# A hybrid decoder block on one core: first input piece in one transfer, 12 idle products, another order list, another order of squares at the join

## Chip, cores and metric

The kernel runs on one core of one Trainium2 chip. The metric is the device time in microseconds of one execution, as the median of the runs. The core's engines are TensorE (PE; its weight loads are shown as PEld), VectorE (DVE), ScalarE (ACT), GpSimd (POOL) and SyncE (SP), which here issues nearly all transfers.

## What is computed

One decoder layer in float32 on x of 256 tokens by 1024. The reference, cut to its frame:

```python
for l in range(DEPTH):                     # DEPTH = 1
    h = rms_norm(x, mix_pre_norm[l])
    mix = hybrid_token_mixer(h, w_in[l], ..., w_out[l], ...)
    x = x + rms_norm(mix, mix_post_norm[l])
    h = rms_norm(x, ffn_pre_norm[l])
    x = x + rms_norm(conv_glu_ffn(h, w_up[l], ffn_conv_w[l], ffn_conv_b[l], w_down[l]), ffn_post_norm[l])
```

The mixer projects h once and splits the columns into three groups of heads: sliding-window attention with sinks, block attention (one block of 256 here, so plain causal attention with ALiBi), and a gated delta rule with a short convolution on q, k and v, whose chunk needs the inverse of a unit lower triangular matrix. The three outputs are joined and go through w_out. The feed-forward part is up-projection (2 x 2816 columns), a convolution of width 3, GeGLU and down-projection.

## The kernel before

**Split products.** Every large product is made of three: each operand is split into a high part (rounded to the type fp32r, by ACT) and a low part (the rest, by VectorE), and hi x hi, hi x lo and lo x hi are summed in PSUM (`passes`). So each weight that arrives must be cast by ACT and then subtracted by VectorE before TensorE can use it.

**The start.** SP loads the transposed x together with the first weights (values of both attentions and the gates, 392 columns) in four pieces `fx[0]` to `fx[3]`, each with two of the eight k-tiles; `fx[0]` comes in two transfers, one per k-tile (L206, L207), the others whole (L209). The norm's weights `pre` come by their own transfer on ACT's queue (L200). While they are on the way TensorE runs WARM = 16 products of a tile of ones with itself (`idle`, L282), whose result nobody reads. Then, for each k-tile, ACT makes the high part of x times `pre` (L292) and of the weights (L293), VectorE the low parts (L294, L296), and TensorE sums them into `pb` (L302), k-tiles 0 and 1 first, then 2 and 3, and so on.

**The mixer.** The rest of the mixer is written as short generators: `n` is the first norm (its last product `p_r`, L331, and the copy `rbc`, L333, which every projection's evacuation needs), `g0` to `g11` are the delta rule's projections (four steps of 6 products, L354, then evacuation, convolution and tanh), `a0` to `a6` those of the attentions, `z0` and `z1` the output gates, `lX` loads of weights and `sX` their splits (L223 and L227; `so` are those of w_out), `i` and `j` the two parts of the triangular inverse (short, dependent steps on VectorE, ACT and TensorE), `r`, `f`, `w`, `s`, `u` the delta rule's products with it, `o0` and `o1` its outputs with their norm, `p`, `N`, `T` and `v` scores, normalising, turning and the value products of the attentions, `t` the turning of the delta rule's outputs, `O` the products of w_out: `O8` is its k-tile 4 for the first 128 tokens, and the two steps of one O are the two halves of 512 columns. A list of 645 steps, PLAN, says in which order these steps are issued; `g0*2` means two steps of g0. Under the manual schedule each engine works its instructions off in the order of that list, so a step that waits holds up what stands behind it on its engine. Some last steps of w_out (`w_rest`) are held back to fill the join.

**The join.** When all of w_out for the first 128 tokens is summed in two halves `pm[0][0]` and `pm[0][1]`, ACT squares each half and sums the squares (`post_sq`, L988), VectorE multiplies it by the norm's weights (`post_w`, L991); `resid` makes the root (`rms_scale`: the sum's scaling L87 and L89, ACT's root L91, the reciprocal L95), adds x, squares again, and `norm_transpose` weighs and turns the result (L164), on which the up-projection starts. Then follows the same for the other 128 tokens.

**The feed-forward part** (`load_up`, `up_products`, `up_gate`, `down`) streams 33 MB of weights. It isn't touched.

## Time and profile before

| | us |
|---|---|
| median of 3 runs (336.42 to 336.85) | 336.52 |
| profiled execution | 335.96 |
| its span, first to last instruction | 334.20 |

| engine | busy us | share of the span |
|---|---|---|
| PE | 321.7 | 96% |
| PEld | 296.4 | 89% |
| DVE | 264.0 | 79% |
| ACT | 212.8 | 64% |
| POOL | 2.4 | 1% |

The profile is that of one execution. The busy share is a mean over stages that have different limits, so it is read by stage: which engine is full in a stretch, and which wait ends last there. An instruction's row gives its start, how long it took, the engine, the line, the operation with the tiles written and read, and in brackets how long the engine stood idle before it and what ended that. Matmuls overlap: one that took 0.39 us may follow the one before by 0.23 us. A plain float32 product of 128 columns is recorded as two matmuls, a transpose as one. The granted clock was 0.993 of full speed as a mean.

### The profile page before, as it was taken

How to read it: one execution, taken by the hardware profiler on the slowest of the kernel's cores; microseconds unless marked ns; L12 is line 12 of the kernel's file. 1: busy time of each engine (PE TensorE's matmuls, PEld its weight loads, DVE VectorE, ACT ScalarE, POOL GpSimd, SP SyncE). 2: the span in 40 equal slices, each digit the busy share in tenths (PEclk: the TensorE clock that was granted, in tenths of full speed). 3: DMA queues.
4: the chain of work that ended last, by engine and by line, in shares of the span. 5: the costliest groups of instructions: out<-in, count | busy, mean ns of one | idle time of the engine just before them, and what ended most of it. 6: DMA issues, size and time to landing. Idle time of an engine off the chain costs nothing.

```text
...
## 1 busy us (share of the span) xinstructions
PE 321.7 (96%) x2500; PEld 296.4 (89%) x2500; DVE 264.0 (79%) x596; ACT 212.8 (64%) x457; POOL 2.4 (1%) x11
## 2 busy tenths in 40 slices
...
GB/s 271 420 354 273 102 233 126 127 93 99 25 355 240 15 140 347 79 127 49 206 127 232 334 315 246 176 210 250 128 234 146 251 127 126 127 126 2 0 61 64
DMA packets 9821, 58.18 MB, mean 174 GB/s; under 512 B 1472, under 2 KB 1728, under 8 KB 3520
## 3 DMA queue, kind: packets, MB, share of 16 engines
...
q10 hardware_dynamic: 144, 0.00, 0.0%
...
## 4 chain that ended last, share of the span: by engine, by line
PE 59%; DVE 26%; ACT 8%; DMA 3%; issue 2%; SPq 1%; DVEq 0%; ACTq 0%
PE pu L181 29%; PE py L187 17%; PE pm L187 7%; DVE cv L372 4%; PE pt L1005 3%; DMA wg_raw<-wg 3%; DVE wg_lo L227 3%; DVE wa_lo L227 2%; DVE u L1036 2%; DVE wz_lo L227 1%; DVE cm L366 1%; ACT wo_hi L223 1%; DVE pr L875 1%; DVE wd_lo L121 1%; DVE U L610 1%
## 5 line engine op out<-in xcount | busy, mean ns | idle before, releaser
L181 PE MATMUL pu<-hT_hi,wu_hi 128*128 128x256 f32 x304 | 84.3, 277 | 0.0
L181 PE MATMUL pu<-hT_lo,wu_hi 128*128 128x256 f32 x304 | 84.1, 277 | 0.0
L181 PE MATMUL pu<-hT_hi,wu_lo 128*128 128x256 f32 x304 | 84.1, 277 | 0.0
L121 DVE TENSOR_TENSOR wu_lo<-wu_raw,wu_hi 128x1024 fp32r<-128x1024 f32 (+1 forms) x54 | 51.7, 983 | 19.8 <-ACT wu_hi L120 19.8
L181 PEld LDWEIGHTS pu<-hT_lo,wu_hi 128*128 128x128 f32 x304 | 57.2, 188 | 0.7
L181 PEld LDWEIGHTS pu<-hT_hi,wu_hi 128*128 128x128 f32 x304 | 57.1, 188 | 0.7
L181 PEld LDWEIGHTS pu<-hT_hi,wu_lo 128*128 128x128 f32 x304 | 57.1, 188 | 0.0
L120 ACT CAST wu_hi<-wu_raw 128x1024 fp32r<-128x1024 f32 (+1 forms) x54 | 44.7, 858 | 16.9 <-PE pu L181 16.9
L1036 DVE SCALAR_TENSOR_TENSOR u<-pu,prm,u 128x255 f32<-128x255 f32 (+1 forms) x88 | 41.1, 477 | 6.3 <-ACT u L1034 5.2
L187 PE MATMUL py<-wd_hi,mT_hi 128*128 128x512 f32 x88 | 34.4, 391 | 0.2 <-ACT wd_hi L120 0.2
L187 PE MATMUL py<-wd_hi,mT_lo 128*128 128x512 f32 x88 | 34.5, 392 | 0.0
L187 PE MATMUL py<-wd_lo,mT_hi 128*128 128x512 f32 x88 | 34.3, 394 | 0.0
L131 ACT CAST mT_hi<-ge 128x256 fp32r<-128x256 f32 x22 | 8.9, 406 | 32.8 <-DVE ge L1040 32.8
L121 DVE TENSOR_TENSOR wd_lo<-wd_raw,wd_hi 128x1024 fp32r<-128x1024 f32 (+1 forms) x28 | 27.1, 987 | 1.3 <-ACT wd_hi L120 1.3
L1034 ACT ACTIVATE u<-pu,prm 128x256 f32<-128x256 f32 x44 | 24.2, 560 | 5.4 <-PE pu L181 5.4
L120 ACT CAST wd_hi<-wd_raw 128x1024 fp32r<-128x1024 f32 (+1 forms) x28 | 22.8, 865 | 2.9 <-DMA wd_raw<-wd 2.9
L354 PE MATMUL pg<-hT_hi,wg_hi 128*128 128x256 f32 x96 | 24.1, 287 | 0.2 <-ACT wg_hi L223 0.2
L354 PE MATMUL pg<-hT_lo,wg_hi 128*128 128x256 f32 x96 | 23.2, 277 | 0.0
L187 PEld LDWEIGHTS py<-wd_hi,mT_hi 128*128 128x128 f32 x88 | 16.5, 188 | 3.4 <-ACT wd_hi L120 0.4
L187 PEld LDWEIGHTS py<-wd_lo,mT_hi 128*128 128x128 f32 x88 | 16.5, 188 | 3.3
L187 PEld LDWEIGHTS py<-wd_hi,mT_lo 128*128 128x128 f32 x88 | 16.5, 188 | 3.1
L354 PEld LDWEIGHTS pg<-hT_hi,wg_hi 128*128 128x128 f32 x96 | 18.1, 188 | 0.7 <-ACT wg_hi L223 0.4
...
## 6 DMA issues: line engine op xcount, KB each, us to landing
...
```

What stands on the lines that cost most here:

```text
L120: A.copy(hi[:, b:e], raw[:, c + b:c + e])
L121: V.tensor_tensor(lo[:, b:e], raw[:, c + b:c + e], hi[:, b:e].bitcast(F32), ALU.subtract)
L131: return A.copy(hi, src), V.tensor_tensor(lo, src, hi.bitcast(F32), ALU.subtract)
L181: T.matmul(pt[:, :S], x[:, k * P:(k + 1) * P], h[:, k, :], start=(i == 0), stop=(i == 3 * KT - 1))
L187: T.matmul(acc[n][j], y[:, ms], x[:, c], start=(first and i == 0), stop=(last and i == 2))
L223: A.copy(hi[:, :step], raw[:, b:b + step])
L227: V.tensor_tensor(lo[:, :step], raw[:, b:b + step], hi[:, :step].bitcast(F32), ALU.subtract)
L354: T.matmul(pt[:, :S], x[:, k * P:(k + 1) * P], h[:, k, :], start=(k + j == 0), stop=(k + 1 == KT and j == 2))
L372: V.scalar_tensor_tensor(t[:, s:], m[:, :S - s], cw[:, c, 3 - s:4 - s], t[:, s:], ALU.mult, ALU.add)
L1005: T.matmul(pt[:, :256], h[:, 4 * j + k, n * P:(n + 1) * P], x[:, k * 256:(k + 1) * 256], start=(j + s + k == 0), stop=(j + s + k == 6))
L1034: A.activation(t, pu[c][:, :S], AF.Identity, scale=fw[:, c, 2:3], bias=fw[:, c, 3:4])
L1036: V.scalar_tensor_tensor(t[:, s:], pu[c][:, :S - s], fw[:, c, 2 - s:3 - s], t[:, s:], ALU.mult, ALU.add)
```

## The change

Four things change.

- The input array `fx` gets the norm's eight weights as its first columns; the first piece comes in one transfer of 8 + 2 x 648 columns and `pre` is a view of it. The transfer on ACT's queue is gone.
- WARM is 12 in place of 16.
- PLAN is another order of the same 645 steps: every step stands in both lists equally often.
- At the join ACT's square and VectorE's weighing of half 0 come first, then the square of half 1; the weighing of half 1 is done inside `rms_scale`, between ACT's root and the reciprocal. (`some(SP[0])`, which stood there, splits nothing, as SP[0] is 0.)

In `pair_split` the low tile is entered in the store when it is made, not after the subtraction; the instructions are the same. The diff, the list cut to its beginning and end:

```diff
-la0 l*3 sg0*3 n sg0 n g1 n g0 n*2 g1 n*4 g0 sg2 n*2 x*2 g1 x n V sg2 g0 sg2 g1 n V lg4 sg2 G g0 sa0 g3 G*3 sa0 c n g3 n
-c g2 G*2 sa0 g0 G g1 g3 G g0 G sa0 g2 g1 lg6 g3 sg4 g0 g2 G g1 g0 a0 G sg4*2 g2 g5 g0 G sg4 g0 a0 g5 g0 la2 g2 a0 G g1
-g2 g5 G g1 g2 g1 g4 g3 G g2 g5 G g1 g4 G g2 g3 G*2 g2 a0 g3 G g2 g4 g3 lg8 sa2 G a0 a1 g3 S sa2*2 g4 a1 g3 S g4 sg6 g3
-a2 S sa2 g4 k0 g6 k0 S g5 k0 k1 k0 sg6 lg10 k0 g6 sg6 a2 g4 k1 sg6 k1 g6 k1*2 g5 L0 K g4 S*2 sg8 K g5 g6 K g4 D0 L1 K
...
-g9 g11 i Q0 Q1 Q0 g9 Q0 z1 i Q0 g8 g9 i a1 Q1 g11 g10 g9 z1 Q1 i Q1 g10 g11 z0 i g10 Q1 i a3 g10 i g10 z0 sz0 a3 i la6
-g10 z1 i sz4*2 sa4 z0 z1 i sz4 z0 z1 i Q1 i g11 lo4 z0 i g11 z1 i g11 z0 i g11 a1 i p1 g11 i Q0 i p0 i p0*2 z1 i p0*2 i
-p1 p0 r0 i p0 p1 a4 i p0 p1 i r1 r0 A1 p1 a4 i p1 r1 r0 i sa4 z1 p1 r0 z0 r0 r1 p1 r1 a4 i r1 N0 i p1 i z0 i N0 i sa4
-N0 i a4 N0 i N0 z0 A1 i*2 sa6 N0 i N0*2 z1 N0 T1 N0*2 i T0 z1 so4 a3 N0 a4 i T0 A1 T1 a6 z0 T3 i a6 sa4 v0 i*4 lo6 sa6
-j v0 T2 j*2 a6 j so4 j a5 T2 so4 a6 j*2 v0 a5 j so4 j T3 j so6 lo0 a6 v1 j*3 so6*2 j v1 so6 p3 j v1 j p3 so0 lo2 a5
-p3*4 a3 j p3*2 a5 so0*2 f p3 a5 w so0 f o0 w f a3 o0*3 p2 o0 f o0*4 s o0 p2 o0 p2*2 o0 p2*2 o0*2 p2*2 u o0 p2 o0*3 s N1
-o0 u o1 N1 u N1 u N1 u N1 T4 N1*2 T5 o1 T4 N1 T5 T6 N1 o1 o0 v2 o1 o0 o1*4 T7 T6 o1*2 v2 o1 T7 o1 v2 o1 v3 o1*7 t0 o1
-v3 t1 o1 t2 t0 v3 t1 t0 t3 t2 t1 O9 t3 t2 t3 O9 O11*2 O8*2 O10 so2 O10 so2 O12 so2 O12 so2 O0*2 O2*2 O4*2 O6*2 O14*2
-O13 O15 O1 O3 O5 O7
+la0 l*3 sg0*3 n g0 sg0 n g1 n g1 n*2 g1 n g1 n*3 sg2 g0 n*2 x*3 g0 n V sg2*2 g2 g0 n V lg4 sg2 G sa0 g2*2 G*3 sa0 c g2
+n sa0 g3 n g3 g0 G c sa0 g0 g3 lg6 sg4 g3 g1 G*2 g0 g1 a1 G g0 g4 g1 G g0 g4 g1 g0 G a1 g2 g0 a1 G g1 g2 G sg4*2 a1 la2
+a0 g1 G a1 g4 g1 G g3 g4 G sg4 g3 g5 G g5 g3 G g2 g5 G*2 g2 g5 G g3 lg8 sa2 g2 a0 g3 g2 g4 a0 g3 g2 g5 a0 g4 G g3 g4 S
+g5 k0 a0 L0 S g4 k0*2 S b k0 k1 k0 g4 L1 k1 g5 k1 S k1 sa2 a2 k1 g4 S a2 S sa2 K g4 a2 K g5 D0 K sa2 a3 sg6 a2 D0 K g5
...
+sz4*2 z1*2 la6 sa4 i g7 z1 i g7 z1 i g7 g9 i g11 p0 i p0 g8 g11 i g8 g11 i g8 i g11 g8 p1 i p1*2 z0 i p1 g8 i z0 p1 g9
+i g7 p1 z0 g9 i g9 Q1 i p1 A1 Q1 i g9 Q1*2 i A0 N0 Q1 sz4 g9 N0 p1 g10 i A1 lo4 z1 i N0 A0 z1 Q1 N0 z0 i g9 i N0 z0 i
+N0 i N0 T0 i z0 g10 N0 i T0 T1 i z1 Q0 N0*2 T1 i N0*2 Q0 g10 Q0 T2 Q0 sa4 a4 i g10 i Q0 sa4 g11 g10 a4 i g11 g10 a5 sa6
+i*4 g11 a5 g10 so4 j g11 a4 Q0 g11 g10 j a4 j g10 j sa4 j T3 g11 v0 j lo6 j*3 g11 j a4 T2 sa6 v0 T3 a5 j*2 r1 j r0 v0
+r1 j r1 so4 r1*2 r0*2 a5 z1 r0 j lo0 z0 a6 r0 so4 a5 j so6 so4 p2 j so6*2 w p2 so6 p2 f lo2 so0 p2 a6 f w a6 p2*2 so0
+p2 a6 so0 o0 p2 a6 p2 f so0 o0*3 p3 o0 f o0*3 s o0*2 p3 o0 p3*2 o0 p3*2 o0*2 p3*2 u o0 s o0*2 p3 o0 o1 o0 u o0 u o0 u
+N1 v1 u N1*2 o1 N1 o1 T4 N1 o1 N1 T5 N1 o1 N1 o1 T6 N1 T4 o1*2 v1 T7 o1 T5 o1 v1 o1 v2 o1*7 T6 o1*2 v2 t0 o1 T7 t1 v2
+t0 v3 o1 t1 t0 t1 t3 v3 O8 t3 v3 O9 t3 O11 t2 O10 t2 O9 t2 O11 O12 O0 O2 O8 O10 so2 O12 so2*2 O0 O2 so2 O4*2 O6 O14 O6
+O14 O13 O15 O1 O3 O5 O7
 CH_F = 256
 FL = 6
 TM = 3
-WARM = 16
+WARM = 12
 LATE = 5
 SP = [0, 0, 4, 4]
 
@@ -196,17 +196,16 @@
         kp = mctx.enter_context(tc.tile_pool(name="kp", bufs=2))
         mctx.enter_context(tc.manual_schedule())
 
-        pre = mp.tile([P, KT], F32, name="pre")
-        nc.scalar.dma_start(pre, a["pre"])
         ones = mp.tile([P, P], F32, name="ones")
         G.memset(ones, 1.0)
 
-        fx = [mp.tile([P, 2 * (S + W_BVA)], F32, tag=t, name=f"fx{k}") for k, t in enumerate(("R", "gb", "DL", "L"))]
         FW = S + W_BVA
-        nc.sync.dma_start(fx[0][:, :FW], a["fx"][:, 0, :FW])
-        nc.sync.dma_start(fx[0][:, FW:], a["fx"][:, 0, FW:])
+        fx = [mp.tile([P, (KT if k == 0 else 0) + 2 * FW], F32, tag=t, name=f"fx{k}")
+              for k, t in enumerate(("R", "gb", "DL", "L"))]
+        nc.sync.dma_start(fx[0], a["fx"][:, :KT + 2 * FW])
+        pre = fx[0][:, 0:KT]
         for k in range(1, KT // 2):
-            nc.sync.dma_start(fx[k], a["fx"][:, k, :])
+            nc.sync.dma_start(fx[k], a["fx"][:, KT + 2 * k * FW:KT + 2 * (k + 1) * FW])
 
 
         raws = {}
@@ -220,12 +219,11 @@
             raw = raws.pop((key, c))
             for b in range(0, w, step):
                 hi = wp.tile([P, 1024], F32R, tag="hi", bufs=HL, name=f"{key}_hi{c}{b}")
+                part = store[c * cols // 1024 + b // step] = [hi, None]
                 A.copy(hi[:, :step], raw[:, b:b + step])
-                part = store[c * cols // 1024 + b // step] = [hi, None]
-                yield
-                lo = wp.tile([P, 1024], F32R, tag="lo", bufs=HL, name=f"{key}_lo{c}{b}")
+                yield
+                lo = part[1] = wp.tile([P, 1024], F32R, tag="lo", bufs=HL, name=f"{key}_lo{c}{b}")
                 V.tensor_tensor(lo[:, :step], raw[:, b:b + step], hi[:, :step].bitcast(F32), ALU.subtract)
-                part[1] = lo
                 yield
 
         wz, wg, wa, wo = {}, {}, {}, {}
@@ -287,7 +285,8 @@
             w.append((hi, lo))
             for b in range(2):
 
-                k, x, y = 2 * j + b, fx[j][:, b * FW:b * FW + S], fx[j][:, b * FW + S:(b + 1) * FW]
+                k, o = 2 * j + b, (KT if j == 0 else 0) + b * FW
+                x, y = fx[j][:, o:o + S], fx[j][:, o + S:o + FW]
                 c = slice(b * W_BVA, (b + 1) * W_BVA)
                 A.activation(hT_hi[:, k, :], x, AF.Copy, scale=pre[:, k:k + 1])
                 A.copy(hi[:, c], y)
@@ -1074,10 +1073,10 @@
             V.tensor_tensor(lo, src, hi.bitcast(F32), ALU.subtract)
 
     with tc.manual_schedule(engines={V.engine, A.engine, T.engine}):
-        for j in range(2):
-            post_sq(pm[0], sqm[0], "m0", j)
-            post_w(pm[0], wrow[:, 0], x2[0], 1 - j)
-        r = resid(0, lambda: some(SP[0]), lambda: some(SP[1]))
+        post_sq(pm[0], sqm[0], "m0", 0)
+        post_w(pm[0], wrow[:, 0], x2[0], 0)
+        post_sq(pm[0], sqm[0], "m0", 1)
+        r = resid(0, lambda: post_w(pm[0], wrow[:, 0], x2[0], 1), lambda: some(SP[1]))
         w_rest((6, 7, 0, 1))
         pts = norm_transpose(x2[0], r, wpre, xw[0], 0, "n2")
         w_rest((2, 3))
@@ -1188,7 +1187,7 @@
     o["wa"] = cm(w, np.concatenate([hd[0], hd[2], hd[1], hd[3], ar(256, 384), ar(512, 768), ar(768, 1024)]))
     wb = tm(w[:, np.concatenate([ar(384, 512), ar(1024, 1280), ar(3328, 3336)])])
     xT = g["x"][0].reshape(S, KT, P).transpose(2, 1, 0)
-    o["fx"] = np.concatenate([xT, wb], 2).reshape(P, KT // 2, -1)
+    o["fx"] = np.concatenate([pp(g["mix_pre_norm"][0]), np.concatenate([xT, wb], 2).reshape(P, -1)], 1)
     o["wz"] = tm(w[:, 2816:3328])
     o["wo"] = tm(g["w_out"][0])
     o["wd"] = tm(g["w_down"][0])
@@ -1202,7 +1201,6 @@
     o["prm"] = np.ascontiguousarray(np.concatenate(
         [cwt.reshape(P, -1), fwt.reshape(P, -1), pp(g["dn_norm"][0])], 1))
     o["row"] = np.concatenate([g["swa_sinks"], g["dn_a_log"], g["dn_dt_bias"]], 1)
-    o["pre"] = np.ascontiguousarray(pp(g["mix_pre_norm"][0]))
     o["post"] = np.ascontiguousarray(np.stack([g["mix_post_norm"][0], g["ffn_pre_norm"][0]])[None])
     o["last"] = g["ffn_post_norm"]
     o["x"] = np.ascontiguousarray(g["x"][0])
```

In the list, the first step of i stands at place 267 before and 239 after, the first of j at 459 and 435, the last of f at 527 and 524, the last of o1 at 604 in both. The projections g10 and g11 have their first step at 244 and 269 before and at 246 and 319 after, their last at 331 and 360 before and at 444 and 456 after; r0 and r1 end at 399 and 405 before and at 485 and 475 after; z0 and z1 end at 447 and 437 before and at 483 and 479 after.

## Rows read from the trace of the kernel before

**Rows 1.** Stages: stretch, length, busy us by engine, clock, DMA, GB/s

```profile
20.00:80.00 60.00, 59.47 (x470) 56.24 (x470) 59.83 (x178) 44.83 (x118) 0.65 (x3) 1.00 0.50 175
...
90.90:110.60 19.70, 18.46 (x207) 16.70 (x205) 16.43 (x50) 15.58 (x43) 0.00 (x0) 1.00 0.74 266
110.60:119.40 8.80, 6.88 (x44) 4.42 (x45) 7.09 (x31) 6.66 (x23) 0.00 (x0) 1.00 0.00 1
...
152.60:327.40 174.80, 174.59 (x1260) 163.17 (x1260) 131.52 (x211) 104.39 (x171) 0.00 (x0) 1.00 0.46 166
```

**Rows 2.** The start, by engine: start, us, engine, line, tiles

```profile
1.01 5.99 PE L282 MATMUL idle<-ones 128*128 128x128 f32 x32 [1.01 <-POOL ones L202]
6.75 0.60 PE L302 MATMUL pb<-wb_hi,hT_hi 128*128 128x392 f32 x2
...
9.65 0.30 PEld L302 LDWEIGHTS pb<-wb_hi,hT_hi 128*128 128x128 f32 x2 [0.47 <-ACT wb_hi L293]
...
4.19 0.51 ACT L292 ACTIVATE hT_hi<-fx,pre 128x256 fp32r<-128x256 f32 x1 [1.54 <-DMA pre<-pre]
...
7.86 0.51 ACT L292 ACTIVATE hT_hi<-fx,pre 128x256 fp32r<-128x256 f32 x1 [1.93 <-DMA fx<-fx]
```

**Rows 3.** Idle products alone, two stretches: busy us, records

```profile
3.00:5.20 2.20, 2.20 (x12) 2.20 (x12) 1.00 0.99 384
5.60:6.70 1.10, 1.10 (x12) 1.10 (x11) 1.00 1.01 339
```

**Rows 4.** Transfers of fx, and one stretch of the start

```profile
DMA to landing us min/median/max: 3.3/6.2/8.5
...
6.40:7.90 1.50, 1.50 (x12) 1.50 (x11) 0.18 (x1) 0.04 (x1) 0.00 (x0) 1.00 0.98 363
```

**Rows 5.** First projections and the copy rbc, in order of time

```profile
14.65 2.36 DVE L227 TENSOR_TENSOR wg_lo<-wg_raw,wg_hi 128x1024 fp32r<-128x1024 f32 x2 [0.91 <-ACT wg_hi L223]
...
16.00:19.00 3.00, 3.00 (x28) 1.00 1.00 423
...
22.13 0.61 PE L331 MATMUL p_r<-dg,ones 128*128 128x128 f32 x4
...
23.98 0.42 DVE L333 COPY rbc<-p_r 128x256 f32<-128x256 f32 x1
```

**Rows 6.** Waits from 90 to 111 us, VectorE's first and last of four

```profile
DVE Ef L686 <- ACT D L684: 0.8, 1, 0.8
...
DVE w1St L757 <- PE p_S L755: 0.6, 1, 0.6
```

**Rows 7.** Last chain before w_out, in order of time

```profile
110.61 1.16 PE L813 MATMUL p_o<-Yt,DL 128*128 128x128 f32 x8 [0.55 <-ACT Yt L776]
...
112.22 0.69 DVE L817 TENSOR_TENSOR oq<-p_o,oq 128x512 f32<-128x512 f32 x1 [0.16 <-PE pp L910]
...
113.02 0.84 ACT L913 COPY pT<-pp 128x384 f32<-128x384 f32 x2
...
113.75 0.32 ACT L823 ACTIVATE jo<-oq 128x128 f32<-128x128 f32 x1
...
115.06 0.16 DVE L826 SCALAR_TENSOR_TENSOR fv<-sso,ssq_q 128x4 f32<-128x4 f32 x1 [1.17 <-ACT jo L823]
...
118.10 0.85 PE L839 MATMUL p_ot<-cst,zg 128*128 128x128 f32 x5 [0.88 <-DVE zg L833]
...
119.41 0.48 PE L187 MATMUL pm<-wo_hi,mT_hi 128*128 128x512 f32 x1
```

**Rows 8.** The join, by engine, in order of time

```profile
134.17 0.60 ACT L988 ACTIVATE m0jk<-pm 128x512 f32<-128x512 f32 x1 [0.73 <-DVE x L991]
...
135.33 0.16 DVE L95 RECIPROCAL m_r<-m_s 128x1 f32<-128x1 f32 x1 [0.27 <-ACT m_s L91]
...
145.57 0.68 DVE L991 TENSOR_TENSOR x<-pm,wrow 128x512 f32<-128x512 f32 x1
...
140.33 1.29 PE L164 MATMUL n_p<-cst,xw 128*128 128x128 f32 x8
```

More of the change, by code (lines that the diff above doesn't have):

```diff
@@ L37 @@
 PLAN = """
-la0 l*3 sg0*3 n sg0 n g1 n g0 n*2 g1 n*4 g0 sg2 n*2 x*2 g1 x n V sg2 g0 sg2 g1 n V lg4 sg2 G g0 sa0 g3 G*3 sa0 c n g3 n
-c g2 G*2 sa0 g0 G g1 g3 G g0 G sa0 g2 g1 lg6 g3 sg4 g0 g2 G g1 g0 a0 G sg4*2 g2 g5 g0 G sg4 g0 a0 g5 g0 la2 g2 a0 G g1
-g2 g5 G g1 g2 g1 g4 g3 G g2 g5 G g1 g4 G g2 g3 G*2 g2 a0 g3 G g2 g4 g3 lg8 sa2 G a0 a1 g3 S sa2*2 g4 a1 g3 S g4 sg6 g3
-a2 S sa2 g4 k0 g6 k0 S g5 k0 k1 k0 sg6 lg10 k0 g6 sg6 a2 g4 k1 sg6 k1 g6 k1*2 g5 L0 K g4 S*2 sg8 K g5 g6 K g4 D0 L1 K
-g5 D0 g4 g6 D0 g8 lz0 K g5 D0 K g4 g5 g7 K b g6 g8 K g6 K d0 g5 g6 g7 d0 K sg8 d0 a2 d0*2 sg8 g7 g6 K g8 K d0 sg8 g6 a2
@@ L43 @@
-sg10 g8 K g6 lz4 h*2 L0 D1 g7 L0 D1 L0 D1 L0 d1 D1 a2 a1 A0 d1*2 g9 g7 d1*2 sg10 g7 g10 d1 g9 sg10 g7 L1 g10 g7 L1 sz0
-g9 g7 sg10 g10 g7 g9 g8 la4 L1 g8 g10 L1 g9 i*2 g11 i*2 g8 p0 i g8 i g8 i g7 g11 g10 sz0 g9 A0 g8 sz0 g9 g11 A0 Q0 sz4
-g9 g11 i Q0 Q1 Q0 g9 Q0 z1 i Q0 g8 g9 i a1 Q1 g11 g10 g9 z1 Q1 i Q1 g10 g11 z0 i g10 Q1 i a3 g10 i g10 z0 sz0 a3 i la6
-g10 z1 i sz4*2 sa4 z0 z1 i sz4 z0 z1 i Q1 i g11 lo4 z0 i g11 z1 i g11 z0 i g11 a1 i p1 g11 i Q0 i p0 i p0*2 z1 i p0*2 i
-p1 p0 r0 i p0 p1 a4 i p0 p1 i r1 r0 A1 p1 a4 i p1 r1 r0 i sa4 z1 p1 r0 z0 r0 r1 p1 r1 a4 i r1 N0 i p1 i z0 i N0 i sa4
```

3 lines of the change are left out of this document (added).

## The prediction

> **What bounds the kernel now.** Read first the table of stages [rows 1]: for each stretch of the span it has the busy time of each engine. Most of it is bound by TensorE: from 152.6 to 327.4 us PE is busy 174.59 of 174.80 us, and no part of the change reaches that stretch. What can move lies ahead of it. From 20 to 80 us two engines are full, PE with 59.47 and VectorE with 59.83 of 60.00 us; VectorE never waits there, so it sets the pace of the mixer. From 90.9 to 110.6 us VectorE has 16.43 of 19.70 us, so 3.27 us of waits; from 110.6 to 119.4 us, where the delta rule's outputs are normed and turned, it has 7.09 and PE 6.88 of 8.80 us. At 119.41 us the first w_out product starts [rows 7]; behind it PE works through to the join, which costs it 0.6 us [rows 8]. So a change ahead of that product moves the end by as much as it moves that product. Second, I read the start in order of time [rows 2 to 5], third VectorE's waits after 90 us [rows 6], fourth the last chain before w_out [rows 7], last the join [rows 8].
>
> The sum is made against the profiled execution, 335.96 us with a span of 334.20 us; the median of the three runs shown is 336.52 us, 0.56 us above, and the saving is taken from that median.
>
> **The change, part by part.**
>
> *Refactored splits.* Storing the lo tile earlier in `pair_split` issues the same instructions in the same order: nothing.
>
> *Idle products.* 16 products are 32 records from 1.01 to 7.00 us [rows 2]. Up to 5.2 us twelve records take 2.2 us, after 5.6 us twelve take 1.1 us [rows 3]: TensorE goes from 1.2 to 2.4 GHz while it is busy with them, though the clock column shows 1.00 throughout. The eight records taken away lie at the fast end, about 0.11 us each, so PE is free 0.9 us earlier, at 5.85 us for 6.75 us. That is still behind the rise, so the rest should run fast as before. The Trainium skill (TensorE: Matmul & The Clock Gate, Part 1) says that the point of the rise differs from run to run; one trace can't show that, and a rise later than 5.5 us would by the page cost part of these 0.9 us.
>
> *First piece whole.* ACT's first step on it waited for the norm's weights until 4.19 us [rows 2]; that separate transfer goes, and with it the two halves. ACT then read the second half without a wait, so all of it had landed by about 5.0 us; the whole piece lands between 4.2 and 5.0 us, and I take 4.7. ACT's cast of the first weights is ready 0.9 us later, at 5.6 us: in time for PE at 5.85 us. Cover: the 12 idle products. Without them the later landing would cost 0.5 us.
>
> *What the start gives.* The first 12 real products take 2.2 us, until about 8.1 us. The next need the second piece. It reached ACT at 7.86 us, after a wait of 1.93 us, and PE went on at 9.65 us, once ACT had cast the weights of that piece's second half [rows 2]. Does it land earlier? It lands 6.2 us after its issue, the middle of the five transfers of fx (3.3 to 8.5) [rows 4]. Meanwhile the engines moved 363 GB/s [rows 4], so the pipe was full and single packets of that piece were late. Landing as before, the 0.9 us become a wait and PE still goes on at 9.65 us: gain 0. Landing in turn, at about 6.5 us (the first piece's 4.7 and 648 KB at 363 GB/s), PE goes on at 8.5 us: 1.2 us earlier. I take neither end.
>
> The Trainium skill (DMA: Bandwidth & Descriptors, Latency and other measured facts) says that two of the sixteen DMA engines are usually slower than the rest. By that rule the second piece stays late and the start gives 0; without it 1.2 us. The late landing agrees, but no view here shows the engines one by one.
>
> *The order list, early.* Nothing is added: 645 steps in both lists. Old and new have 18 VectorE steps ahead of the copy `rbc` (last step of n), but PE's product before it, p_r, now stands behind 12 projection steps instead of 9. A step is 6 products; 28 in 3.00 us is 0.11 each [rows 5], so p_r comes 3 x 6 x 0.113 = 2.0 us later. Before, p_r ended at 22.74 us and the copy began at 23.98: a slack of 1.24 us [rows 5]. So VectorE waits 0.8 us if PE starts as before, and not at all if it starts 0.8 us or more earlier. VectorE's own start at 14.65 us hangs on ACT's cast of the first wg transfer [rows 5]; that may come up to 0.8 us earlier with the late packets gone. From +0.8 to -0.8; I take +0.3, as rows 2 lean to the late landing.
>
> *The order list, middle.* The inversion (i) begins as the 239th step, before as the 267th; the second part (j) as the 435th, before 459th, while the step that it feeds, f, ends at 524 and 527. The chain j to f, where VectorE waited, has 90 steps for its length instead of 69, filled with projections g10, g11 and with r0, r1 that ran earlier before. Of the 3.27 us, the four waits of 0.64 to 0.80 us in [rows 6] are 2.9 us: each is one link of that chain. Between nothing and all of 2.9 goes; I take half, -1.5, because ACT's long casts (so4, so6) still stand between links. In 20 to 80 us, where VectorE had no wait, a reordered list can only add: from 0 to 2; I take +0.8, one wait of the size in rows 6. Besides, three VectorE steps now come after p_o (a low part of 0.4, an output of 0.3, a reciprocal of 0.1): -0.8.
>
> *The order list, last chain.* From p_o (110.61) over the sum oq (112.22), the squares (from 113.75), the sum's use (115.06) to the turning at 118.10 us and w_out at 119.41 [rows 7]. p_o ended at 111.77, so the sum was 0.45 us late, behind normalising steps; after it ACT made two pT copies before the squares, 0.84 us; VectorE then waited 1.17 us. The new list has two normalising steps after the reciprocal ahead of the sum instead of six, the squares ahead of the copies, and fills the wait with what is left. Upper end: 0.45 + 0.84 and 0.4 for w_out starting after the first turning, with t2 behind the first w_out steps, so 1.7; lower end 0, if v2 and v3, which still stand ahead, become late. I take -1.1.
>
> *The join.* Before, ACT's second square waited 0.73 us for VectorE, which read the same half of pm; VectorE went on with the reciprocal at 135.33 us [rows 8]. Now half 0 is finished two steps (6 products of 0.228, 1.4 us) before half 1, squared and weighed meanwhile; the square of half 1 starts at once: -0.7. The weighing of half 1 moves in front of the reciprocal; the other tile's row shows that weighing, 0.68 us from 145.57 [rows 8], against an idle of 0.27: +0.25. Net -0.45 on the chain to the turned tiles. PE had 1.29 us for 8 transposes of 0.11 and 0.22 before them [rows 8], 0.6 us idle, so it takes the 0.4: -0.4 (0 to -0.45). The tile's second chain, already so ordered, stays.
>
> **Sum:** 0.3 - 1.5 + 0.8 - 0.8 - 1.1 - 0.4 = -2.7 us. That makes 333.3 us for the profiled execution and **333.8 us** for the median.
>
> **Rivals.**
> - *The start comes whole.* The second piece lands in turn, p_r and the first wg come earlier: -0.8 in place of +0.3, so -3.8: 332.7 us. For it: fewer transfers ahead, a full pipe. Against it: the 1.93 us wait of rows 2.
> - *The waits only change place.* VectorE bounds from 14.65 us; ACT's casts between the links stay, and the chain j waits as long (0 for -1.5), the last chain gives half. +0.3 + 0.8 - 0.8 - 0.55 - 0.4 = -0.65: 335.9 us. For it: both lists hold the same VectorE work.
> - *Slower: PE too far back in the list.* The new list puts more PE work ahead of the VectorE steps that use it. If the projections late in the list (g10, g11, z0, z1, each begun over 130 steps before its last) let VectorE run dry between 20 and 80 us, each us counts in full: p_r's 0.8 and 3.3 us of such waits, with -0.8 for the three steps, -0.7 in the last chain, -0.4 at the join and nothing from the chain j, make +2.2: 338.7 us. It decides from about 3.5 us of such waits on, if all else comes as summed (0.8 are in the sum). Against it: the margin is short before the copy `rbc` alone; later on more VectorE work stands between a projection and its use in both lists.
> - *The list does nothing and the join alone comes:* -0.4, within what can be told: 336.1 us.
>
> **How the numbers follow.** Forecast 0.46, whole start 0.20, changed place 0.15, join alone 0.04, slower 0.15. A measurement of this kernel tells 0.2%, about 0.7 us, from no change. The first two are faster, with the near side of the third: 0.70; the rest of third and fourth: 0.15; slower 0.15. The range goes from the forecast with the upper ends of start and middle (-5.3 us, 331.2) to +0.4 us, 336.9, which leaves out most of the slower case.
>
> **What will show it.** Right: VectorE's waits between 90 us and the first w_out product fall from 5.0 to under 3 us, that product starts at 117 us or earlier, the reciprocal of the join comes 0.7 us after its m_w, and the two squares of the join have no wait for VectorE. The start: PE's first real product at 5.9 us, and the landing of the second piece tells which rival holds. Wrong: waits of VectorE between 20 and 80 us, above all at `rbc`; a clock that rises after the idle products; squares of oq still behind copies; or other waits in the chain j of the same length.

## The result, and the profile after

| | before | after |
|---|---|---|
| median of 20 runs each, us | 336.58 | 333.45 |
| lowest and highest run, us | 335.45, 340.46 | 332.42, 338.00 |
| profiled execution, us | 335.96 | 336.45 |
| its span, us | 334.20 | 334.3 |

The ratio of after to before is 0.9929, with a 95% interval of 0.9904 to 0.9954: about 2.4 us faster, between 1.5 and 3.2; by the medians 3.1. Forecast were 333.8 us and a gain of 2.7. One sentence is needed to read the profile: from 180 us on, the up-projection's products follow each other at 0.118 us in some of the traced executions, that of after among them, and at 0.113 us in the others, that of before among them, which makes 3 to 4 us. So the ends of the two traces say nothing, and they are compared up to the first product behind the join (142.85 us before, 139.34 after).

**Stages** (as [rows 1]: stretch, length, busy us by engine, clock, DMA, GB/s), kernel after:

```profile
20.00:80.00 60.00, 59.04 (x461) 56.00 (x460) 58.53 (x182) 41.26 (x107) 1.00 (x3) 1.00 0.48 172
90.90:110.60 19.70, 18.96 (x171) 17.02 (x171) 18.74 (x57) 17.08 (x52) 0.00 (x0) 1.00 0.69 260
110.60:119.40 8.80, 6.99 (x44) 4.89 (x44) 6.10 (x26) 5.43 (x20) 0.00 (x0) 1.00 0.00 0
```

The busy times are those of PE, PEld, DVE, ACT and POOL. In 20 to 80 us VectorE (DVE) now has 1.47 us without work (0.17 before), in 90.9 to 110.6 us 0.96 us (3.27 before). Its waits from 18 us to 120 us, total, times, longest, kernel after:

```profile
DVE mT_lo L842 <- ACT mT_hi L840: 1.8, 1, 1.8
DVE wa_lo L226 <- ACT wa_hi L223: 0.5, 2, 0.3
DVE g_y L424 <- DMA row<-row: 0.5, 1, 0.5
DVE fv L825 <- ACT jo L822: 0.5, 1, 0.5
DVE Ef L685 <- ACT D L683: 0.4, 1, 0.4
DVE wo_lo L226 <- ACT wo_hi L223: 0.2, 1, 0.2
```

The first of these lies behind the start of w_out, where nothing hangs on it. Of the four waits of 0.6 to 0.8 us in the chain j [rows 6], Ef is left with 0.4 and wo_lo with 0.2. New between 20 and 80 us are wa_lo and g_y, 1.0 us, of which 0.8 us lie ahead of the copy `rbc`.

**The start**, by engine (as [rows 2]), kernel after:

```profile
1.01 4.57 PE L280 MATMUL idle<-ones 128*128 128x128 f32 x24 [1.01 <-POOL ones L200]
5.74 0.62 PE L301 MATMUL pb<-wb_hi,hT_hi 128*128 128x392 f32 x2 [0.16 <-ACT wb_hi L292]
...
7.99 0.89 PE L301 MATMUL pb<-wb_hi,hT_hi 128*128 128x392 f32 x4
...
4.77 0.51 ACT L291 ACTIVATE hT_hi<-fx 128x256 fp32r<-128x256 f32 x1 [2.55 <-DMA fx<-fx]
...
6.42 0.51 ACT L291 ACTIVATE hT_hi<-fx,fx 128x256 fp32r<-128x256 f32 x1
```

The whole first piece is read at 4.77 us. The second is there when ACT asks for it at 6.42 us, without a wait; before, ACT waited for it until 7.86 us [rows 2]. PE goes on without a gap. Further on (as [rows 5]):

```profile
13.19 2.36 DVE L226 TENSOR_TENSOR wg_lo<-wg_raw,wg_hi 128x1024 fp32r<-128x1024 f32 x2 [0.78 <-ACT wg_hi L223]
...
22.92 0.61 PE L330 MATMUL p_r<-dg,ones 128*128 128x128 f32 x4
...
23.56 0.42 DVE L332 COPY rbc<-p_r 128x256 f32<-128x256 f32 x1
```

VectorE begins 1.46 us earlier (14.65 before), PE's p_r stands later in the list and yet the copy `rbc` has no wait; but p_r ends only 0.03 us ahead of it.

**The last chain** (as [rows 7]), by engine, kernel after:

```profile
107.38 1.16 PE L812 MATMUL p_o<-Yt,DL 128*128 128x128 f32 x8
...
114.62 0.59 PE L838 MATMUL p_ot<-cst,zg 128*128 128x128 f32 x3 [0.90 <-DVE zg L832]
115.14 0.87 PE L923 MATMUL pv<-pT,va 128*64 128x256 f32 x8
...
116.14 0.48 PE L187 MATMUL pm<-wo_hi,mT_hi 128*128 128x512 f32 x1
...
107.31 1.12 DVE L832 SCALAR_TENSOR_TENSOR zg<-p_o,f_r,zg 128x128 f32<-128x128 f32 x4
...
109.04 0.68 DVE L816 TENSOR_TENSOR oq<-p_o,oq 128x512 f32<-128x512 f32 x1
...
111.57 0.16 DVE L825 SCALAR_TENSOR_TENSOR fv<-sso,ssq_q 128x4 f32<-128x4 f32 x1 [0.47 <-ACT jo L822]
...
108.87 1.28 ACT L103 ACT_TABLE_LOAD   x1
110.16 0.20 ACT L103 ACTIVATE warm<-den 128x1 f32<-128x1 f32 x1
110.27 0.29 ACT L822 ACTIVATE jo<-oq 128x128 f32<-128x128 f32 x1
```

The first w_out product starts at 116.14 us, 3.27 us earlier than before. Nearly all of that is there at p_o already (107.38 for 110.61, 3.23 us). The sum oq ended at 109.72, yet the squares begin at 110.27: ACT loads a table first. And w_out follows the turning of 114.62 us by 1.52 us (1.31 before). From 90 us to the first w_out product VectorE is busy 24.33 of 26.14 us, so its waits are 1.8 us.

**The join** (as [rows 8]), by engine, kernel after:

```profile
129.04 0.60 ACT L987 ACTIVATE m0jk<-pm 128x512 f32<-128x512 f32 x1 [2.49 <-PE pm L187]
...
130.41 0.60 ACT L987 ACTIVATE m0jk<-pm 128x512 f32<-128x512 f32 x1 [0.69 <-PE pm L187]
...
131.32 0.20 ACT L91 ACTIVATE m_s<-m_w 128x1 f32<-128x1 f32 x1 [0.23 <-DVE m_w L89]
...
131.13 0.16 DVE L89 SCALAR_TENSOR_TENSOR m_w<-msq,m_w 128x1 f32<-128x1 f32 x1 [0.62 <-ACT m0jk L987]
131.21 0.69 DVE L990 TENSOR_TENSOR x<-pm,wrow 128x512 f32<-128x512 f32 x1
131.81 0.15 DVE L95 RECIPROCAL m_r<-m_s 128x1 f32<-128x1 f32 x1
```

The second square waits for TensorE alone, and the reciprocal follows m_w by 0.68 us, with half 1's weighing between.

### The profile page after: what moved, and what is told of

It reads as the page before. It is cut to its first block, busy times and chain, and to the rows that moved or that the text cites. A ratio compares the mean times of both kernels' runs of the same rounds, so it can differ in the third digit from the quotient of the medians.

```text
span 334.3 us, 6407 instructions
## 1 busy us (share of the span) xinstructions
PE 322.7 (97%) x2492; PEld 298.6 (89%) x2492; DVE 264.5 (79%) x596; ACT 211.9 (63%) x457; POOL 2.8 (1%) x11
## 4 chain that ended last, share of the span: by engine, by line
PE 76%; DVE 13%; ACT 7%; issue 2%; DMA 1%; DVEq 0%; ACTq 0%
PE pu L181 30%; PE py L187 17%; PE pm L187 7%; PE pg L353 6%; PE pz L785 3%; PE pt L1004 3%; PE pb L301 3%; PE pa L353 3%; DVE wg_lo L226 2%; DVE u L1035 2%; DMA fx<-fx 1%; DVE wo_lo L226 1%; DVE wd_lo L121 1%; ACT L103 1%; DVE wa_lo L226 1%
## 5 line engine op out<-in xcount | busy, mean ns | idle before, releaser
L181 PE MATMUL pu<-hT_hi,wu_hi 128*128 128x256 f32 x304 | 85.7, 282 | 0.0
L181 PE MATMUL pu<-hT_hi,wu_lo 128*128 128x256 f32 x304 | 85.6, 281 | 0.0
L181 PE MATMUL pu<-hT_lo,wu_hi 128*128 128x256 f32 x304 | 85.5, 281 | 0.0
L181 PEld LDWEIGHTS pu<-hT_hi,wu_lo 128*128 128x128 f32 x304 | 58.3, 192 | 0.0
```

The lines of the kernel that those rows point to most:

```text
L181: T.matmul(pt[:, :S], x[:, k * P:(k + 1) * P], h[:, k, :], start=(i == 0), stop=(i == 3 * KT - 1))
```

## The experiments

The theory on record with the first runs was that the parts add up, as in the sum; the rival, that the same waits stand behind each part, so that a lead at the start is lost again before w_out. Shifts against before, in us, from the traces (minus is earlier):

| point | after | start_only | list_only | join_only |
|---|---|---|---|---|
| second piece at ACT | -1.4 | -1.4 | 0.0 | -0.3 |
| copy rbc | -0.4 | -1.0 | +1.0 | -0.4 |
| chain i done (Xt) | -3.6 | -0.9 | -2.1 | -0.3 |
| chain j, last Ef | -4.6 | -0.2 | -2.3 | +0.5 |
| p_o | -3.2 | -0.2 | -0.9 | +0.5 |
| first w_out product | -3.3 | -0.2 | -1.0 | +0.5 |
| first product behind the join | -3.5 | -0.2 | -0.7 | +0.1 |

**start_only**: first piece and 12 idle products, old list and join.

```diff
-WARM = 16
+WARM = 12
...
-        nc.sync.dma_start(fx[0][:, :FW], a["fx"][:, 0, :FW])
-        nc.sync.dma_start(fx[0][:, FW:], a["fx"][:, 0, FW:])
+        nc.sync.dma_start(fx[0], a["fx"][:, :KT + 2 * FW])
+        pre = fx[0][:, 0:KT]
```

> The kernel before with the first piece whole and 12 idle products, old list, old join. Theory A (the start carries through, since VectorE has no wait after it and starts earlier too): first real product at 5.7 us for 6.75, first projection near 14.4 us for 15.85, VectorE's first wg split near 13.2 us for 14.65, first w_out product at 118.0 us for 119.4, time 1.2 to 1.4 us below before. Rival B (the mixer's list swallows it): the first projection is earlier all the same, but the first w_out product stays within 0.3 us of 119.4 and the time within 0.4 us of before.

Measured: 336.91 us, ratio 0.9992 [0.9952, 1.0032]; the interval goes from 1.6 us faster to 1.1 us slower, so by the time neither theory is excluded. In the trace the lead of 1.4 us at ACT is 1.0 us at the copy `rbc` and 0.9 us at Xt. At the last Ef 0.2 us of it are left; in between PE paused, of which more below.

**list_only**: the new list in the kernel before.

```diff
-la0 l*3 sg0*3 n sg0 n g1 n g0 n*2 g1 n*4 g0 sg2 n*2 x*2 g1 x n V sg2 g0 sg2 g1 n V lg4 sg2 G g0 sa0 g3 G*3 sa0 c n g3 n
+la0 l*3 sg0*3 n g0 sg0 n g1 n g1 n*2 g1 n g1 n*3 sg2 g0 n*2 x*3 g0 n V sg2*2 g2 g0 n V lg4 sg2 G sa0 g2*2 G*3 sa0 c g2
...
```

> The kernel before with the new order list alone: two transfers for the first piece, 16 idle products, old join. Theory A: the list gives what the start doesn't, 1.7 to 2.2 us below before, the first w_out product near 117.4 us; the copy rbc waits, as p_r stands three projection steps later, and comes 0.5 to 1.0 us after 23.98. Rival B (the list alone makes the gain): 2.8 to 3.4 us below before, first w_out product at 116.1.

Measured: 335.57 us, ratio 0.9953 [0.9920, 0.9985], in time near theory A; the first w_out product came 1.0 us earlier, not the 2.0 of theory A. The copy waits for p_r, as the forecast had it for a late start (0.8):

```profile
24.94 0.42 DVE L333 COPY rbc<-p_r 128x256 f32<-128x256 f32 x1 [0.58 <-PE p_r L331]
```

**join_only**: the new join in the kernel before.

```diff
-        for j in range(2):
-            post_sq(pm[0], sqm[0], "m0", j)
-            post_w(pm[0], wrow[:, 0], x2[0], 1 - j)
-        r = resid(0, lambda: some(SP[0]), lambda: some(SP[1]))
+        post_sq(pm[0], sqm[0], "m0", 0)
+        post_w(pm[0], wrow[:, 0], x2[0], 0)
+        post_sq(pm[0], sqm[0], "m0", 1)
+        r = resid(0, lambda: post_w(pm[0], wrow[:, 0], x2[0], 1), lambda: some(SP[1]))
```

> The kernel before with the new order at the join alone; the old list still ends both halves of pm one step apart, so half 0 is ready 0.7 us before half 1. My step of the prediction: the join's reciprocal 0.45 us earlier on the chain with the new list; here, with half 0 ready later, 0.2 to 0.45 us, and time 0.1 to 0.4 us below before. Rival: the chain isn't what PE waits for (its 1.29 us for 8 transposes stay), time within 0.1 us of before.

Measured: 336.46 us, ratio 0.9975 [0.9950, 0.9999]. From the first w_out product to the first product behind the join it took 23.10 us instead of 23.43.

By the traces the three shifts at the first w_out product add up to -0.7 us, where the whole change has -3.3. By the times it can't be said: the product of the three ratios is 0.992, and their intervals are wide. What is missing in the traces is for the most part a pause of PE inside one row of 64 short products of the chain, of list_only first, then of after:

```profile
84.78 0.72 PE L642 MATMUL p_D<-Dc,Y 32*32 32x32 f32 x60
86.22 0.25 PE L642 MATMUL p_D<-Dc,Y 32*32 32x32 f32 x4 [0.72 <-issue]
```

```profile
83.36 0.75 PE L641 MATMUL p_D<-Dc,Y 32*32 32x32 f32 x64
```

"issue" means that PE waited for nothing that the trace shows. VectorE's next step (Dc) waited 1.0 us for it in list_only. All three single parts had this pause (0.6 to 0.7 us); before and after had not. It belongs to the execution: up to there join_only gives PE the same work as before. What it costs shows where the way from the copy `rbc` to w_out is cut into stretches, in us:

| stretch | before | start_only | join_only | list_only | after |
|---|---|---|---|---|---|
| copy rbc to Xt | 58.66 | 58.77 | 58.78 | 55.56 | 55.48 |
| Xt to last Ef | 18.72 | 19.43 | 19.48 | 18.55 | 17.71 |
| last Ef to p_o | 9.24 | 9.24 | 9.24 | 10.63 | 10.63 |
| p_o to first w_out product | 8.81 | 8.82 | 8.82 | 8.76 | 8.76 |

Under one list three of the stretches take the same time whatever the start. The second is longer where PE pauses. So it is in all traces: under the new list 18.42 and 18.55 us with the pause and 17.59 to 18.01 us without; under the old one 19.30 to 19.48 us with it, and 18.72 us in before, the only trace there without it. The pause thus takes 0.7 to 0.8 us from each of the three parts, 2.3 us in all; without it they would add up to -3.0 us at w_out, near the -3.3 of the whole change. The traces bear out the theory: the parts add up, and a shift at the copy `rbc` reaches w_out.

**after_again**: the changed kernel once more, unchanged.

> The changed kernel again. The profiled execution of it on record ran the 256-column products of the up-projection at 0.117 us each, the kernel before at 0.113; if that pace belongs to an execution and not to the change, some executions here have 0.113, their time is near 333.0 us, the first w_out product near 116 us and the last product 3.3 to 3.6 us earlier than before. If it belongs to the change, all have 0.117.

Measured: 336.66 us, ratio 0.9959 [0.9927, 0.9992]; ten of twelve executions lay between 336.29 and 337.06 us, two at 334.4 us, none near the 333.0 that was looked for. The first w_out product came 0.2 us later than in after's trace, so the mixer's gain is repeated; the products have 0.118 us in this trace too, and that pace makes the time. The rows that show it are the first and the last of ten products that follow each other without a gap, of after and then of after_late_table (below):

```profile
182.63 0.28 PE L181 MATMUL pu<-hT_hi,wu_hi 128*128 128x256 f32 x1
...
183.69 0.28 PE L181 MATMUL pu<-hT_hi,wu_hi 128*128 128x256 f32 x1
```

```profile
182.01 0.28 PE L181 MATMUL pu<-hT_hi,wu_hi 128*128 128x256 f32 x1
...
183.03 0.28 PE L181 MATMUL pu<-hT_hi,wu_hi 128*128 128x256 f32 x1
```

Nine steps in 1.06 us (0.118 each) and in 1.02 (0.113). No kernel was traced at both paces. But kernels with the old list have either (before 0.113, start_only 0.118), those with the new list too, and the twenty times of after fall into two groups, 332.42 to 335.04 and 336.45 to 338.00 us, so the change isn't what sets the pace.

**after_warm16**: 16 idle products in the changed kernel.

```diff
-WARM = 12
+WARM = 16
```

> The changed kernel with 16 idle products again. Theory (the new list leans on an early PE): PE's first real product 0.9 us or so later than in the changed kernel, first projection near 15.3 us for 14.2; VectorE's first wg split stays at 13.2 us, so the copy rbc now waits for p_r, 0.5 us or more, and the first w_out product comes 0.5 to 1.0 us later than in the changed kernel; time 0.5 to 1.0 us above it. Rival (the idle products only fill a wait): time within 0.3 us of the changed kernel.

Measured: 334.65 us, ratio 0.9941 [0.9916, 0.9966]; after's median was 333.45, the lowest runs 333.25 and 332.42. In the trace the first real product came 0.3 us later than in after, at 6.00 us, not the 0.9 expected; with twelve products it came at 6.16 us in after_old_join. So no cost of the four products is shown. Behind that stand a wait of 0.8 us at cv, a pause in p_D (VectorE waits 0.8 us at Dc) and a fall of the clock at the end of the last chain, which may have come by the execution.

**after_split12**: the changed list and join with 12 idle products, but halves and a transfer of their own for the weights, as before.

```diff
-        nc.sync.dma_start(fx[0], a["fx"][:, :KT + 2 * FW])
-        pre = fx[0][:, 0:KT]
+        pre = mp.tile([P, KT], F32, name="pre")
+        nc.scalar.dma_start(pre, a["pre"])
+        nc.sync.dma_start(fx[0][:, :FW], a["fx"][:, 0, :FW])
+        nc.sync.dma_start(fx[0][:, FW:], a["fx"][:, 0, FW:])
```

> The new list, the new join and 12 idle products, but the first piece in two transfers and the norm's weights by their own, as before. In both kernels run so far with the two transfers the second piece reached ACT 1.4 us later than in those with one. Theory (the whole piece is what brings the second piece in time, and the list needs that): second piece at ACT near 7.8 us, PE idle about 1 us before it, first projection at 15.6 us or later, first w_out product near 118 us, time 1.8 to 2.6 us above the changed kernel at the same pace of the products. Rival (the 12 idle products do it): time within 0.5 us of the changed kernel.

Measured: 333.64 us, ratio 0.9902 [0.9863, 0.9941], no other than after. Against what was thought, the second piece came early here too (read 0.2 us later than in after). And the clock fell at the end of the last chain; columns as in the stages, after_split12 and then after:

```profile
112.00:115.00 3.00, 1.68 (x12) 0.93 (x12) 2.59 (x15) 1.99 (x6) 0.00 (x0) 1.00 0.00 0
115.00:118.00 3.00, 2.91 (x14) 1.86 (x15) 2.12 (x8) 1.36 (x4) 0.00 (x0) 0.53 0.00 0
```

```profile
112.00:115.00 3.00, 2.01 (x15) 1.20 (x15) 2.69 (x14) 1.67 (x5) 0.00 (x0) 1.00 0.00 0
115.00:118.00 3.00, 3.00 (x20) 2.27 (x20) 2.37 (x7) 1.68 (x4) 0.00 (x0) 1.00 0.00 0
```

TensorE was busy for 1.68 of 3.00 us before the fall, waiting for the norm; at the lower level (1.2 GHz) it has 14 products in the next 3 us, where after has 20. But in after_old_join it was busy for the same 1.68 us in that stretch and the clock stayed at 1.00, so what sets off the fall isn't shown. From p_o to the first w_out product it took 9.86 us for 8.76 in after, and from p_o to the transposes of the join 31.19 for 29.71: the fall cost 1.5 us.

**after_old_join**: the changed kernel with the join of before (join_only's edit, undone).

```diff
-        post_sq(pm[0], sqm[0], "m0", 0)
-        post_w(pm[0], wrow[:, 0], x2[0], 0)
-        post_sq(pm[0], sqm[0], "m0", 1)
-        r = resid(0, lambda: post_w(pm[0], wrow[:, 0], x2[0], 1), lambda: some(SP[1]))
+        for j in range(2):
+            post_sq(pm[0], sqm[0], "m0", j)
+            post_w(pm[0], wrow[:, 0], x2[0], 1 - j)
+        r = resid(0, lambda: some(SP[0]), lambda: some(SP[1]))
```

> The changed kernel with the old order at the join. By the prediction the new order is worth 0.4 us: the join's reciprocal 0.4 to 0.5 us later after the last product of half 1, ACT's second square waiting for VectorE again, the up-projection 0.3 to 0.5 us later. Rival: 0 to 0.1 us, since PE has other products in the join.

Measured: 333.68 us, ratio 0.9899 [0.9853, 0.9944]. In the trace the stretch from the first w_out product to the first product behind the join is 23.68 us, in after 23.21: the new join is worth 0.47 us there; in time the two aren't told apart. The square waits for VectorE again:

```profile
131.70 0.60 ACT L987 ACTIVATE m0jk<-pm 128x512 f32<-128x512 f32 x1 [1.41 <-DVE x L990]
```

**after_late_table**: the table for the root is loaded behind the last turned tile instead of ahead of the squares of oq.

```diff
-    warm(cp, AF.Sqrt, den[:, H - 1, 1:2], "warm0")
+    warm(cp, AF.Sqrt, mT_hi[:, KT - 1, 0:1].bitcast(F32), "warm0")
```

> The changed kernel with ACT's table load for the join's root (1.28 us, and 0.20 us for the idle root after it) moved from in front of the squares of oq to behind the turned tiles. Theory (that load is why the last chain gained 0.3 us and not the 1.1 forecast): the squares start within 0.2 us of the end of the sum oq instead of 0.6 us after it, the first turning comes 0.5 us earlier after p_o, and the first w_out product 0.3 to 0.5 us earlier; time 0.2 to 0.5 us below the changed kernel. Rival (w_out waits for v3 and the last turnings anyhow): first w_out product and time within 0.15 us.

Measured: 332.60 us, ratio 0.9886 [0.9825, 0.9948], the lowest median of all. PE, ACT and VectorE:

```profile
115.72 0.48 PE L187 MATMUL pm<-wo_hi,mT_hi 128*128 128x512 f32 x1
...
109.83 0.31 ACT L822 ACTIVATE jo<-oq 128x128 f32<-128x128 f32 x1 [0.90 <-DVE oq L816]
...
116.50 1.28 ACT L103 ACT_TABLE_LOAD   x1
...
111.14 0.16 DVE L825 SCALAR_TENSOR_TENSOR fv<-sso,ssq_q 128x4 f32<-128x4 f32 x1
```

The sum ended at 109.80 (109.11 and 0.69); the squares follow by 0.03 us instead of 0.55, VectorE no longer waits for them (0.47 in after), and w_out starts 0.42 us earlier than in after. The table load stands where ACT has nothing due. From p_o to w_out all three kernels with the late load take 8.27 us, after 8.76. Five of the six runs lie at 332.30 to 332.81 us. In time it is faster than before; from after it isn't told apart, as the intervals of the two ratios overlap.

The last four kernels ask what of the first piece does what: the whole piece, or the weights without ACT's transfer. Two readings were open: the second piece, and the time outside the span (time less span), which was 2.15 us in all kernels with the changed piece and 1.79 us in the others.

**late_whole_own_pre**: after_late_table, the piece whole, the weights by their own transfer.

```diff
-        nc.sync.dma_start(fx[0], a["fx"][:, :KT + 2 * FW])
-        pre = fx[0][:, 0:KT]
+        pre = mp.tile([P, KT], F32, name="pre")
+        nc.scalar.dma_start(pre, a["pre"])
+        nc.sync.dma_start(fx[0], a["fx"][:, 0, :])
```

> The changed kernel with the late table load of after_late_table, the first piece whole, but the norm's weights by their own transfer on ScalarE's queue again. Outside the span every kernel whose weights lie in the first piece showed 2.15 us, every kernel with halves and weights apart 1.79 us. If that 0.36 us hangs on ScalarE's queue having no transfer, 1.8 us here and about 332.2 us in time, 0.35 below after_late_table; if it hangs on the whole first piece, 2.15 us and 332.6 us. Second piece at ScalarE near 6.2 us if the whole first piece or the 12 idle products are what brings it, near 7.6 us if the separate transfer of the weights delays it.

**after_halves_pre_in**: after, with two transfers, the weights in the first.

```diff
-        nc.sync.dma_start(fx[0], a["fx"][:, :KT + 2 * FW])
+        nc.sync.dma_start(fx[0][:, :KT + FW], a["fx"][:, :KT + FW])
+        nc.sync.dma_start(fx[0][:, KT + FW:], a["fx"][:, KT + FW:KT + 2 * FW])
```

> The changed kernel with the first piece in two transfers, the norm's weights in the first of them, none on ScalarE's queue. Outside the span 2.15 us if the transfer on ScalarE's queue decides, 1.8 us if the whole piece does. First piece at ScalarE about 3.7 us in place of 4.5 us; second piece at 6.3 us as in after_split12, or 7.6 us if two transfers ahead of it delay it. The time follows only if the second piece comes late: about 333.0 us with it early, 333.6 to 334.4 us with it late.

**late_split12**: after_late_table with the start of after_split12.

```diff
-    warm(cp, AF.Sqrt, den[:, H - 1, 1:2], "warm0")
+    warm(cp, AF.Sqrt, mT_hi[:, KT - 1, 0:1].bitcast(F32), "warm0")
...
+        nc.scalar.dma_start(pre, a["pre"])
+        nc.sync.dma_start(fx[0][:, :FW], a["fx"][:, 0, :FW])
+        nc.sync.dma_start(fx[0][:, FW:], a["fx"][:, 0, FW:])
```

> The changed kernel with the late table load of after_late_table, and the first piece in two transfers with its own transfer of the norm's weights, as before the change; 12 idle products. Outside the span 1.79 us. If the form of the first piece brings nothing, 332.2 to 332.6 us, the merged piece's 0.36 us outside the span saved and the rest as after_late_table (332.6); if the whole piece brings the second one early, 7.6 us at ScalarE and 333 to 334 us. In after_split12 it came at 6.3 us, in one execution.

**warm12_only**: before, with 12 idle products.

```diff
-WARM = 16
+WARM = 12
```

> The kernel before with 12 idle products in place of 16, nothing else. If the second piece's landing hangs on the two halves, it reaches ScalarE near 7.6 us as before, TensorE waits for it and the time stays at 336.5 us. If it came early in after_split12 because of the 12 products, near 6.3 us here too, first projection about 14.4 us for 15.6 us, and yet 336.0 to 336.5 us in time, as start_only lost the same lead by the end of the middle chain.

Measured, with ACT's steps on the pieces under the table:

| kernel | us | ratio | outside the span |
|---|---|---|---|
| late_whole_own_pre | 332.97 | 0.9862 [0.9818, 0.9905] | 2.13 to 2.19 |
| after_halves_pre_in | 333.65 | 0.9874 [0.9822, 0.9925] | 1.77 to 1.82 |
| late_split12 | 334.17 | 0.9890 [0.9837, 0.9943] | 1.74 to 1.83 |
| warm12_only | 338.59 | 1.0015 [0.9972, 1.0057] | 1.75 to 1.84 |

The first step on fx[0] in late_whole_own_pre:

```profile
5.37 0.51 ACT L291 ACTIVATE hT_hi<-fx,pre 128x256 fp32r<-128x256 f32 x1 [2.72 <-DMA pre<-pre]
```

On both pieces in after_halves_pre_in:

```profile
3.81 0.51 ACT L292 ACTIVATE hT_hi<-fx 128x256 fp32r<-128x256 f32 x1 [1.59 <-DMA fx<-fx]
...
7.91 0.51 ACT L292 ACTIVATE hT_hi<-fx,fx 128x256 fp32r<-128x256 f32 x1 [2.36 <-DMA fx<-fx]
```

On the second piece in late_split12, then in warm12_only:

```profile
6.13 0.51 ACT L292 ACTIVATE hT_hi<-fx,pre 128x256 fp32r<-128x256 f32 x1 [0.54 <-DMA fx<-fx]
```

```profile
7.87 0.51 ACT L292 ACTIVATE hT_hi<-fx,pre 128x256 fp32r<-128x256 f32 x1 [1.95 <-DMA fx<-fx]
```

What follows. Apart, the weights landed later than the whole piece itself (5.37 us for 4.77 in after), which cost the lead that was hoped for. Three of late_split12's six executions, 334.12 to 334.84 us, had a mean clock of 0.988 to 0.992, as where the clock falls at the end of the last chain (0.991 in the three traces that show it); its lowest run, 331.93 us, is the lowest of all. The time outside the span hangs on the whole piece, not on ACT's queue: 0.35 us that no row of a trace shows. The second piece was never late behind a whole first piece (7 of 7 traces, start_only's among them; in late_whole_own_pre ACT asked for it at 7.02 us) and late behind halves in 5 of 7, whether the weights lay in them or not; 12 idle products alone don't bring it. Halves don't make it late each time, so these are odds, with one trace for each kernel. And in time the three starts under the new list can't be told apart: after_split12 333.64, after_halves_pre_in 333.65, after 333.45.

## Why the prediction was right, and where not

**Sum.** The forecast was -2.7 us; the medians give -3.1, the ratio's interval -1.5 to -3.2. The sum holds, but in part by luck: its terms were off and stand against each other. In us, from the traces of before and after:

| part | forecast | measured |
|---|---|---|
| start, to the copy rbc | +0.3 | -0.42 |
| middle, copy rbc to p_o | -1.5 | -2.81 |
| last chain, p_o to w_out | -1.1 | -0.05 |
| w_out and join | -0.4 | -0.22 |
| outside the span | 0 | +0.35 |
| sum | -2.7 | -3.15 |

By its own terms the range would begin at -5.2 us, not at -5.3.

*The start.* First real product at 5.9 us: 5.74. First piece taken at 4.7: 4.77. The second piece I left between late and in turn, leaning to late [rows 2, 4]; it came in turn. So the first rival's condition held: no wait at rbc, VectorE 1.46 us earlier at wg. Its price held in part: against before the copy `rbc` came 0.42 us earlier, not 0.8, as g_y and wa_lo waited ahead of it. Between the two ends it held: from list_only to after the copy moved by 1.4 us, where the bounds +0.8 and -0.8 are 1.6 apart, and in after_halves_pre_in, which differs from after in the transfers alone, it is 1.1 us later. By the rule of the Trainium skill (DMA: Bandwidth & Descriptors, Latency and other measured facts) that I weighed, the start would have given 0. But the Trainium skill there puts that slowness down, as a best guess, to transfers that go by GpSimd's path, and those of fx are issued by SP, so it need not have held for them. No run here shows the engines one by one; a second piece that is on time behind every whole first piece speaks against a fixed loss by slow engines.

*Unforecast:* 0.35 us outside the span for the whole piece. I took the diff's merged transfer for free beyond its landing; the trace of before couldn't show it.

*Middle.* The cause was right, the size too small. From the copy `rbc` to p_o VectorE's time without work fell from 3.51 to 1.66 us (forecast -0.7, as -1.5 and +0.8) and its work from 83.12 to 82.16 us (-0.8 for the three steps moved behind p_o). Waits in the chain j fell from 2.9 to 0.6 us (Ef 0.4, wo_lo 0.2): more than the half that I took, -2.3 for -1.5. "New waits" of 0.8 between 20 and 80 us: VectorE is idle there for 1.3 us more than before, 1.0 of it at wa_lo (for ACT) and g_y (for a transfer), most of that ahead of the copy; behind the copy, up to 80 us, it is 0.53 us for 0.11. The slower rival needed 3.5 us of such waits; they stayed far below. At p_o the sum was +0.3 - 1.5 + 0.8 - 0.8 = -1.2 and, with a whole start, -2.3; measured -3.2.

*Last chain.* Forecast -1.1, measured -0.05 (first w_out product -3.27 against p_o's -3.23). This step failed. I had read the two pT copies of ACT, 0.84 us, as what stood ahead of the squares [rows 7], and not the table load and its step ahead of them (1.28 and 0.20 us), ACT's rows in the trace of before:

```profile
111.61 1.28 ACT L103 ACT_TABLE_LOAD   x1
112.91 0.20 ACT L103 ACTIVATE warm<-den 128x1 f32<-128x1 f32 x1
```

The term had three parts. The 0.84 for the copies: they did move behind the squares, but then the table load ended last, 0.55 us after the sum, so 0.3 came. after_late_table took it away: 0.42 us at w_out. The 0.45 for the late sum: it starts 0.50 us after p_o's end (108.54), as four gated outputs zg, 1.12 us from 107.31, now stand ahead of it beside the reciprocal and the two normalising steps; nothing came. The 0.4 for w_out behind the first turning: eight value products (v3), 0.87 us from 115.14, stand between that turning and w_out, the lower end of my bounds; 0.2 was lost.

*Join.* Forecast -0.4; 0.33 us on the old list (join_only), 0.47 on the new one (after_old_join). The whole change shows 0.22, because the new list by itself makes this stretch 0.24 us longer (23.67 us in list_only, 23.43 in before). The mechanism is as put: the square waits for no VectorE, and the reciprocal follows m_w by 0.68 us (0.7). The transposes n_p take 1.03 us from first to last end for 1.29 [rows 8].

*Idle products.* The products went over to the faster pace between 3.9 and 6.9 us in the traces (5.4 in before, 4.4 in after, 6.9 in list_only), in agreement with the Trainium skill (TensorE: Matmul & The Clock Gate, Part 1), by which that point differs from run to run. The Trainium skill there gives half a microsecond either way; the traces show more. In four of the ten traces with twelve products all of them ran at the slower pace, so the step by which twelve end behind the rise held in after, but not in every execution. PE was free before the first piece was cast (a wait of 0.16 us at 5.74). The first real product came 1.0 us earlier than before; how much of that is the four products and how much the earlier rise isn't settled.

**Rivals.** "The waits only change place" is excluded for the list: from the copy `rbc` to w_out it takes 92.6 us for 95.4, with the same 90.0 and 90.2 us of VectorE's work. Nor does it hold for the start: start_only's lead, 1.0 us at the copy, goes where PE pauses, and join_only, which had no new start, lost as much there (0.8 us); after_halves_pre_in's lag of 1.1 us behind after at the copy is 1.1 at p_o. "The join alone" is excluded by list_only's shift of the chain.

**What stays open.** What each part gives in time: the intervals are too wide, and each rests on one trace. What makes the pause, the two paces, the fall of the clock and the late second piece differ from one execution to the next, no run here tells.
